# Row sums of a norm moved to token partitions by small transfers instead of transposes

## The chip, the cores and the metric

The kernel runs on one core of one Trainium2 chip. The metric is the device time of one execution in microseconds; the runs before the change have a median of 970.58 us (970.48 to 973.71, three runs).

## The reference

One encoder layer is applied to two token sequences (256 and 2048 tokens, 1024 features). Cut to what matters here:

```python
h = rms_norm(x, g_pre)
q, k, v, z_a, u_f, z_f = split(h @ w_in)                     # 512 columns each
y_a = neighbourhood_attention(q, k, v, rpb)                  # 8 heads of 64
y_f = fourier_mix(u_f, w_fourier, b_fourier)
mixed = concatenate([rms_norm(y_a, g_na) * silu(z_a), rms_norm(y_f, g_f) * silu(z_f)])
out = mixed @ w_out
return x + rms_norm(out, g_post)

def rms_norm(x, g):                                          # over the features of a token
    return x * rsqrt(mean(x * x, axis=-1) + 1e-6) * g
```

The change concerns the two norms of `y_a` and `y_f`. Each needs, for every one of the 2304 tokens, the sum of 512 squares and from it the factor 1/sqrt(sum/512 + eps).

## The kernel before, in words

The tokens are 18 tiles of 128. Both `y_a` and `y_f` are held with features on partitions and tokens along the row; the squares are added up over four blocks of 128 features into `ysq` (attention) and `sqs` (Fourier part), both 128 x 2304. So the sum over features is a sum over partitions, which TensorE makes with a matmul against ones. The factor is wanted with one token per partition (`invf`, `inva`: 128 x 18, a column for each tile), since the product with `w_out` leaves tokens on partitions and the factor is applied when PSUM is emptied (`f_evac` L1456, `evac` L1675).

The attention stage runs from about 615 to 865 us of the span. Its loop (L1577) runs over 36 groups, k = 2 to 36; the order of every engine is written out by hand, one queue per engine in the order of the code (a manual schedule for ACT, DVE, POOL, SP and PE). One turn of the loop does for group k: the scores on TensorE (L1184), biases and maxima on DVE (L1206), exponentials on ACT (L1211); and for group k-1: transposes of its softmax weights into two PSUM banks `ptb` (`transp`, L1502, which ACT empties at L1510 and DVE at L1512), then at the turn's end the product with v (`pv`, L1517, matmuls L1524). Between them stand the 12 matmuls of a half tile of the Fourier part's product with `w_out` (`f_mm` L1445, L1435), six before and six after the second transposes. At the turn's end SP's queue gets the loads for later groups: v and za of group k+1 (`prep_v`, L1138: L1152, L1154, L1159) and q of group k+3 (`prep`, L1125: L1135). Every DMA of the program is issued from SP's queue but three; eight semaphores are used in turn, so a DMA also waits until the one eight places before it has landed.

The norm's factors are made at eight places in this loop. The table `NT` (L1551) names the turn and the tiles:

```python
NT = {4: range(2, 4), 8: range(4, 8), 10: range(8, 12), 11: range(12, 16), 12: range(16, 18),
      32: range(4), 34: range(4, 8), 36: range(8, 12)}
```

At the end of turn k-1 `norm_sums` (L1479) makes the sums of up to four tiles, each with ones of 32 columns, side by side into 32 rows each of the bank `ptb[0]` (L1482), and ACT copies them to SBUF (L1484). In the middle of turn k, between the first six `w_out` matmuls and the second transposes, `norm_turn` (L1487) transposes that copy on TensorE (L1491), so that each tile's sums become a column, and `rsq_ops` (L1379) makes the factor: logarithm and exponential on ACT (L1381, L1382), and a Newton step on DVE (L1383; L1386 to L1388 a little later, by `run_later`). For k below 32 the factors are `invf`, and from 32 on `inva`.

The last stage (L1738) runs over the 18 tiles: the attention part's product with `w_out`, residual and store. In its second turn (j = 1) `a_norm` (L1495) makes the sums of the last six tiles of `inva`, one matmul pair for each tile with the squares as weights and one column of ones (L1498), which leaves tokens on partitions at once.

Of the kernel before, what the change touches and what calls it, by code (L numbers as in the profile page):

```python
# [10 lines left out]
F32 = mybir.dt.float32  # L11
# [157 lines left out]
def build(tc, A, O):  # L169
    nc = tc.nc  # L170
# [23 lines left out]
    ident = cst.tile([128, 128], F32, name="ident")  # L194
    ones = cst.tile([128, 1], F32, name="ones")
# [7 lines left out]
    invf = cst.tile([128, 18], F32, name="invf")  # L203
    inva = cst.tile([128, 18], F32, name="inva")
# [9 lines left out]
    ps = es.enter_context(tc.tile_pool(name="ps", bufs=3, space=PSUM))  # L214
# [503 lines left out]
    for c in range(3, 6):  # L718
# [7 lines left out]
        if c == 4:  # L726
# [5 lines left out]
            for k in range(KC):  # L732
                for t in range(2):
                    ts = slice(128 * t, 128 * t + 128)
# [25 lines left out]
    for b in range(16):  # L760
# [13 lines left out]
        if 2 <= b < 8:  # L774
            x, y = divmod(b, 2)
# [7 lines left out]
        p = mmt(512)[:, :TP]  # L783
# [3 lines left out]
        o = st.tile([128, 256], F32, tag="f", name="f", bufs=3)  # L787
        if kind % 2:
            i, d = p, o
        else:  # L790
            i = p.rearrange("p (b r c) -> p b r c", b=2, c=32)
# [47 lines left out]
    for i in range(16):  # L839
# [48 lines left out]
        for j in range(7):  # L888
# [29 lines left out]
            if sg == 0:  # L918
                x, y = divmod(7 * (pr - 1) + j, 14)
# [205 lines left out]
    def prep(g):  # L1125
        pr, ts = g["pr"], g["ts"]
        g["qh"] = jl.tile([128, 256], F32R, tag="qh", name="qh", bufs=4)
        g["ql"] = jl.tile([128, 256], F32R, tag="ql", name="ql", bufs=4)
        if g["R"] is None:
            q = qD[pr, :, ts].rearrange("p (b x) -> p b x", b=2)  # L1130
        else:
            sg, x = divmod(g["R"], 2)
            t0 = TP + 1024 * sg + 512 * g["hc"]
            q = qD[pr, :, t0:t0 + 512].rearrange("p (b x) -> p b x", b=2)[:, :, 128 * x:128 * x + 128]
        nc.sync.dma_start(g["ql"].bitcast(F32).rearrange("p (b x) -> p b x", b=2), q)  # L1135
# [243 lines left out]
    def rsq_ops(dst, ssum, n, scale):  # L1379
        l, y, s, t = [sm.tile([128, 8], F32, tag="d" + x, name="d" + x, bufs=1)[:, :n] for x in "lyst"]  # L1380
        nc.scalar.activation(l, ssum, AF.Ln, scale=scale, bias=epst)  # L1381
        nc.scalar.activation(y, l, AF.Exp, scale=-0.5)  # L1382
        V.tensor_scalar(s, ssum, -0.5 * scale, -0.5 * EPS, ALU.mult, ALU.add)  # L1383

        def second():
            V.tensor_tensor(out=t, in0=y, in1=y, op=ALU.mult)  # L1386
            V.tensor_tensor(out=t, in0=t, in1=s, op=ALU.mult)
            V.scalar_tensor_tensor(out=dst, in0=t, scalar=1.5, in1=y, op0=ALU.add, op1=ALU.mult)  # L1388

        later.append(second)  # L1390
# [85 lines left out]

    nsb = []

    def norm_sums(sq, ts):  # L1479
        n = 32 * len(ts)  # L1480
        for x, t in enumerate(ts):
            nc.tensor.matmul(ptb[0][32 * x:32 * x + 32, :128], ones32, sq[:, t * 128:t * 128 + 128], start=True, stop=True)  # L1482
        o = sm.tile([128, 128], F32, name="nsb", bufs=1)[:n]
        nc.scalar.copy(o, ptb[0][:n, :128])  # L1484
        nsb.append(o)

    def norm_turn(dst, ts):  # L1487
        o = nsb.pop()
        n = 32 * len(ts)
        p = ps.tile([128, 128], F32, tag="c", name="pn", bufs=1)[:, :n]  # L1490
        nc.tensor.transpose(p, o, ident[:n, :n])  # L1491
        ts = slice(ts[0], ts[-1] + 1)
        rsq_ops(dst[:, ts], p[:, ::32], ts.stop - ts.start, 1.0 / 512)

    def a_norm(ds):  # L1495
        p = ps.tile([128, 128], F32, tag="c", name="pna", bufs=1)
        for j, d in enumerate(ds):
            nc.tensor.matmul(p[:, j:j + 1], ysq[:, d["t"] * 128:d["t"] * 128 + 128], ones, start=True, stop=True)  # L1498
        n = len(ds)
        rsq_ops(inva[:, ds[0]["i"]:ds[0]["i"] + n], p[:, :n], n, 1.0 / 512)  # L1500

    def transp(g, b):  # L1502
        ch = g["ch"][b]
# [69 lines left out]
    prep_v(G[2])  # L1573
    prep(G[4])
    ones32 = sm.tile([128, 32], F32, name="ones32", bufs=1)
    nc.vector.memset(ones32, 1.0)
    for k in range(2, len(G) + 1):  # L1577
        pr, i = divmod(k, 9)
        g, f = G[k] if k < len(G) else None, G[k - 1] if k else None
        if pr < 3:  # L1580
            if i == 3:
                KK[pr + 1] = load_k(pr + 1)
                for x in range(2):
                    fetch_k(KK[pr + 1], pr + 1, x)
            if i == 7:
                load_t(pr + 1, 0)
        if 0 < pr < 4 and i == 0:
            load_t(pr, 1)
        if pr < 4 and i == 3:
            load_t(pr, 2)  # L1590
        if k == 9:
            nc.sync.dma_start(gpb, pbc(A["gpost"]))
        if k == 23:
            wp = pt.enter_context(tc.tile_pool(name="wp", bufs=1, side="right"))
            WO.extend(wp.tile([128, 4, D], F32R, name="w0%d" % x) for x in range(2))
        if 24 <= k < 32:
            y = k - 24
            nc.sync.dma_start(WO[y % 2][:, y // 2].bitcast(F32), woD[0, y % 2, y // 2])
        x = k // 2 + 1
        if g:  # L1600
            scores(g)
            if 2 < k < 34 and k % 2 == 0:
                ys_mul(ftiles[x])
                if x + 1 < 18:
                    ys_load(ftiles[x + 1])
            bias_max(g, 0, 0)
            exps(g, 0, 0)
            bias_max(g, 0, 1)
            bias_max(g, 1, 0)
        if f:  # L1610
            transp(f, 0)
        if g:
            exps(g, 0, 1)
            bias_max(g, 1, 1)
            exps(g, 1, 0)
            f_mm(k, range(6))
            soft(g, 0)
            exps(g, 1, 1)
        else:
            a_mm(atiles[0], 0, range(6))  # L1620
        if k in NT:
            norm_turn(invf if k < 32 else inva, NT[k])
        if f:
            transp(f, 1)
        if g:
            if k + 1 < len(G):
                split_q(G[k + 1])
            soft(g, 1)
            if k == 2:
                ys_mul(ftiles[x])  # L1630
                ys_load(ftiles[x + 1])
        run_later()
        for v, x0, x1 in YSQ.get(k, []):
            nc.scalar.activation(v[:, x0:x1], v[:, x0:x1], AF.Square)
            V.tensor_tensor(out=sqs[:, x0:x1], in0=sqs[:, x0:x1], in1=v[:, x0:x1], op=ALU.add)
        if g:
            f_mm(k, range(6, 12))
        else:
            a_mm(atiles[0], 0, range(6, 12))
        if pr < 3 and i == 8:  # L1640
            mask_p(pr + 1)
        if k % 2 and x < 18:
            ys_split(ftiles[x])
        if pr < 3 and i in (5, 6, 7, 8):
            split_k(KK[pr + 1], i - 5)
        if k == 34:
            ys_split(atiles[0])
        if g:
            f_evac(k)
        if f:  # L1650
            pv(f)
        if k + 1 in NT:
            norm_sums(sqs if k < 31 else ysq, NT[k + 1])
        if k == 12:
            pq_.close()
        if k + 1 < len(G):
            prep_v(G[k + 1])
        if k + 3 < len(G):
            prep(G[k + 3])
        if k == 28:  # L1660
            xk = [kp.tile([128, T], F32, tag=x, name="xk") for x in ("kh", "kl")]
        if 32 <= k < 36:
            x, d = k - 32, atiles[k - 32]
            d["xt"] = xk[x // 2][:, x % 2 * D:x % 2 * D + D]
            nc.sync.dma_start(d["xt"], A["xn"][d["t"] * 128:d["t"] * 128 + 128, :])
        if k == 32:
            ys_load(atiles[0])
        if k in (34, 35):
            ys_load(atiles[k - 33])
            of_load(atiles[k - 34])  # L1670
        if k == 36:
            ys_split(atiles[1])
# [65 lines left out]
    for j, d in enumerate(atiles):  # L1738
        if j + 3 < 18:
            ys_load(atiles[j + 3])  # L1740
        for x in range(2, 5) if j == 0 else (j + 4,):
            if x < 18:
                of_load(atiles[x])
                if x > 3:
                    xt_load(atiles[x])
        if j:
            a_mm(d, 0)
        if j == 1:
            a_norm(atiles[12:])
            run_later()  # L1750
        a_evac(d, 0)
        if j + 2 < 18:
            y_hi(atiles[j + 2])
        if j == 0:
            for n in range(2):
                nc.scalar.copy(ptb[n], gpb[:, n * 512:n * 512 + 512])
        if j == 17:
            last_tile(d, atiles[16])
            break
        if j:  # L1760
            factor(atiles[j - 1])
            for n in range(2):
                residual(atiles[j - 1], n)
        a_mm(d, 1)
        a_evac(d, 1)
        part_sum(d["sa"])
        guess(d)
        if j + 2 < 18:
            y_lo(atiles[j + 2])
# [16 lines left out]
```

## Time and profile before

| what | value |
|---|---|
| median of the runs | 970.58 us (970.48 to 973.71) |
| the profiled execution: time, span | 971.28 us, 969.5 us |
| mean granted TensorE clock | 0.998 |
| DMA | 279.37 MB in 146382 packets, 288 GB/s |
| attention stage, 615 to 869 us: PE / DVE / ACT / POOL busy | 253.0 / 163.0 / 169.5 / 169.5 of 254.0 us |
| the same stage: share of the DMA engines | 0.86 |
| transposes L1491 | 8, 270 to 273 ns each |
| sums L1482 | 56 matmuls for 28 tiles, 272 to 297 ns each |
| sums L1498 | 12 matmuls for 6 tiles |
| ACT copies L1484 | 8, 247 to 261 ns each |

A float32 matmul that isn't a transpose stands as two instructions in the trace. Durations of matmuls overlap, so the chain of work that ended last tells better than they do what an instruction adds. A row of a timeline is: start in us, length in us, engine, line, operation, tiles written and read, shapes, count, and in brackets the idle time before it with what ended it. For SP's queue (SPq) the length is the time of issuing a DMA, not that of its transfer.

### The profile page before, as it was taken

Reading aid. Unit: us, or ns where it says so; the run is one execution under the profiler, and the core shown is the slowest. Engines: PE = TensorE matmul, PEld = TensorE weight load, DVE = VectorE, ACT = ScalarE, POOL = GpSimd, SP = SyncE. Lnnn points to the kernel's source line nnn. Section 1 sums busy time; section 2 is a strip of 40 time slices with the busy share of each in tenths; the row PEclk is TensorE's granted clock in tenths of the full one; section 3 lists DMA queues with packets and bytes.
Section 4 is the critical chain, followed back from the end, with each engine's and each line's share of the span. In section 5 each row is a group of like instructions: output and inputs, shape, how many; then the busy total and the mean of one; then the engine's idle time right before and its main releaser. Section 6 shows DMA issues by size and latency. Waiting matters only on the chain.

```text
span 969.5 us, 17019 instructions
## 1 busy us (share of the span) xinstructions
PE 959.5 (99%) x5745; PEld 800.4 (83%) x5745; DVE 705.4 (73%) x1306; ACT 496.1 (51%) x1078; POOL 429.8 (44%) x400
## 2 busy tenths in 40 slices
PE   9999999999999999999999999999999999999997
PEld 7889988888888888888888879878787888878886
DVE  6758988687886777797877345776765656649997
ACT  6835676423334533233344256677666676744443
POOL 3100002464751202665655033567677686524544
PEclk9999999999999999999999999999999999999999
DMA  9898796557748997599889898689877998979993
GB/s 334 309 380 316 256 346 245 199 198 261 294 186 353 343 413 258 198 364 344 308 297 333 294 324 328 190 272 297 264 227 249 278 302 283 293 253 324 344 338 133
DMA packets 146382, 279.37 MB, mean 288 GB/s; under 512 B 13730, under 2 KB 84216, under 8 KB 142904
## 3 DMA queue, kind: packets, MB, share of 16 engines
q1 hardware_dynamic: 145864, 277.89, 81.9%
q8 instruction: 46, 0.75, 0.3%
q10 hardware_dynamic: 432, 0.39, 0.1%
q14 instruction: 40, 0.33, 0.1%
HBM read 183.85 MB, written 101.52 MB: 294 GB/s over the span
## 4 chain that ended last, share of the span: by engine, by line
PE 94%; DMA 1%; DVE 1%; SPq 1%; issue 1%; ACT 1%; POOL 1%; DVEq 0%; ACTq 0%; POOLq 0%
PE po L1435 20%; PE mm L165 18%; PE mm L164 17%; PE mm L166 17%; PE pv L1524 5%; PE ptb L1508 5%; PE s L1184 4%; PE pab L1024 2%; DMA ut<-uN 1%; PE py L164 1%; PE py L166 1%; PE py L165 1%; SPq L367 1%; DMA gpre<-gpre 0%; PE ppq L1062 0%
## 5 line engine op out<-in xcount | busy, mean ns | idle before, releaser
L164 PE MATMUL mm<-xh,wa 128*128 128x512 f32 x448 | 174.4, 389 | 0.0
L165 PE MATMUL mm<-xl,wa 128*128 128x512 f32 x448 | 174.3, 389 | 0.0
L166 PE MATMUL mm<-xh,wa 128*128 128x512 f32 x448 | 174.3, 389 | 0.0
L536 POOL TENSOR_TENSOR ws<-wr 128x512 f32<-128x512 f32 x16 | 23.5, 1468 | 228.0 <-DMA wr<-wz 224.0
L1218 POOL TENSOR_SCALAR w<-w,m 128x465 f32<-128x465 f32 (+9 forms) x136 | 85.2, 639 | 44.1 <-DVE m L1215 34.1
L164 PEld LDWEIGHTS mm<-xh,wa 128*128 128x128 f32 x448 | 84.1, 188 | 17.7
L166 PEld LDWEIGHTS mm<-xh,wa 128*128 128x128 f32 x448 | 84.1, 188 | 17.4
L165 PEld LDWEIGHTS mm<-xl,wa 128*128 128x128 f32 x448 | 84.1, 188 | 17.4
L1435 PE MATMUL po<-wo,yh 128*128 128x512 f32 x272 | 90.5, 414 | 0.0
L551 DVE TENSOR_TENSOR wa<-wr,wa 128x512 fp32r<-128x512 f32 x60 | 69.3, 1162 | 27.2 <-ACT wa L550 27.0
L1435 PE MATMUL po<-w,yh 128*128 128x512 f32 x280 | 86.7, 391 | 0.0
L1211 ACT ACTIVATE w<-w,m 128x465 f32<-128x465 f32 (+9 forms) x136 | 78.3, 579 | 15.5 <-DVE m L1206 15.5
L1206 DVE CUSTOM_DVE_ANT_1 w<-s,tb 128x465 f32<-128x465 f32 (+8 forms) x124 | 61.2, 531 | 9.7 <-PE s L1184 9.2
L165 PE MATMUL mm<-vl,xh 128*128 128x512 f32 x168 | 65.6, 390 | 0.2 <-DVE vl L482 0.2
L166 PE MATMUL mm<-vh,xl 128*128 128x512 f32 x168 | 65.4, 389 | 0.0
L164 PE MATMUL mm<-vh,xh 128*128 128x512 f32 x168 | 65.4, 389 | 0.0
L589 POOL TENSOR_TENSOR mt<-mt,rmask 128x880 f32<-128x880 f32 (+2 forms) x24 | 50.8, 2131 | 32.1 <-DVE mt L585 19.8
L877 DVE TENSOR_TENSOR f<-u,mm 128x512 f32<-128x512 f32 x64 | 43.5, 680 | 29.2 <-PE mm L166 24.3
L1435 PEld LDWEIGHTS po<-w,yh 128*128 128x128 f32 x280 | 52.3, 188 | 10.9 <-issue 0.2
L1508 PE MATMUL ptb<-ident,w 128*120 128x128 f32 (+8 forms) x422 | 58.9, 277 | 1.0 <-ACT nsb L1484 0.9
L550 ACT CAST wa<-wr 128x512 fp32r<-128x512 f32 x60 | 36.4, 617 | 44.8 <-PE mm L166 19.3
L1508 PEld LDWEIGHTS ptb<-ident,w 128*120 128x120 f32 (+8 forms) x422 | 47.2, 140 | 13.8 <-issue 8.0
(263 smaller groups left out, 2391.8 us busy)
## 6 DMA issues: line engine op xcount, KB each, us to landing
wr<-wz SPq DMA_DIRECT2D x48, 512.0 KB
vl<-sD SPq DMA_DIRECT2D x20, 512.0 KB
xm<-xm SPq DMA_DIRECT2D x9, 1024.0 KB
oD<-ofs SPq DMA_DIRECT2D x18, 512.0 KB
of<-oD SPq DMA_DIRECT2D x18, 512.0 KB
yr<-yD SPq DMA_DIRECT2D x34, 256.0 KB
zD<-f SPq DMA_DIRECT2D x16, 512.0 KB
woD<-wo SPq DMA_DIRECT2D x16, 512.0 KB
```

The source lines that it names most:

```text
L164: nc.tensor.matmul(out, lh, rh, start=first, stop=False)
L165: nc.tensor.matmul(out, lh, rl, start=False, stop=False)
L166: nc.tensor.matmul(out, ll, rh, start=False, stop=last)
L551: nc.vector.tensor_tensor(out=o[:, 1], in0=src, in1=o[:, 0].bitcast(F32), op=ALU.subtract)
L589: nc.gpsimd.tensor_tensor(out=o, in0=i, in1=rmask[:, m0:m0 + n].unsqueeze(2).to_broadcast([128, n, 80]), op=ALU.add)
L877: nc.vector.tensor_tensor(out=dst(f, b), in0=src(uu[u]), in1=src(p), op=op)
L1206: nc.vector.tensor_tensor_reduce(out=rows(g["w"][b][:, h, :n], w), in0=rows(g["s"][2 * b + h][:, :nr * sw(w)], sw(w))[:, :, :w], in1=tv, s ...
L1211: nc.scalar.activation(w, w, AF.Exp, bias=m[:, h:h + 1], scale=-1.0, accum_out=m[:, 2 + h:3 + h])
L1218: nc.gpsimd.tensor_scalar(w, w, m[:, 4 + h:5 + h], 1.0, ALU.mult, ALU.mult)
L1435: nc.tensor.matmul(p, (d["l"] if x == 2 else d["h"])[:, c], w(n, int(x == 1), c), start=j == 0, stop=j == 11)
L1508: nc.tensor.transpose(ptb[h][:nk, j * 128:j * 128 + 128], g["w"][b][:, h, c0:c0 + nk], ident)
L1524: nc.tensor.matmul(p[hs, b], g["v"][:nk, v, hs], g["pt"][b][:nk, h, j * 128:j * 128 + 128], start=j == 0, stop=j == len(ch) - 1)
```

## The change

The transposes are gone. At the end of turn k-1, behind `prep_v` and `prep`, `norm_turn` issues from SP's queue one DMA for each tile: one row of the copied sums (128 numbers in one partition) goes to a column of a new tile `ssum` (128 x 18), one number for each partition, SBUF to SBUF. In turn k, at the place of the transposes, `norm_root` makes the factor from `ssum`. The last six tiles' sums are made like the others, four in turn j = 1 and two in turn j = 2 of the last stage, each with its copy and its DMAs, and their factor in turn j = 4. There are 34 such DMAs in all. The copy's tile keeps one buffer.

```diff
-    def norm_sums(sq, ts):
+    def norm_sums(sq, ts, p=None):
+        p = ptb[0] if p is None else p
         n = 32 * len(ts)
         for x, t in enumerate(ts):
-            nc.tensor.matmul(ptb[0][32 * x:32 * x + 32, :128], ones32, sq[:, t * 128:t * 128 + 128], start=True, stop=True)
-        o = sm.tile([128, 128], F32, name="nsb", bufs=1)[:n]
-        nc.scalar.copy(o, ptb[0][:n, :128])
-        nsb.append(o)
-
-    def norm_turn(dst, ts):
-        o = nsb.pop()
-        n = 32 * len(ts)
-        p = ps.tile([128, 128], F32, tag="c", name="pn", bufs=1)[:, :n]
-        nc.tensor.transpose(p, o, ident[:n, :n])
+            nc.tensor.matmul(p[32 * x:32 * x + 32, :128], ones32, sq[:, t * 128:t * 128 + 128], start=True, stop=True)
+        o = sm.tile([128, 128], F32, tag="nsb", name="nsb", bufs=1)
+        nc.scalar.copy(o[:n], p[:n, :128])
+        nsb.append((ts, o))
+
+    def norm_turn():
+        while nsb:
+            ts, o = nsb.pop(0)
+            for x, t in enumerate(ts):
+                nc.sync.dma_start(ssum[:, t:t + 1], o[32 * x:32 * x + 1, :])
+
+    def norm_root(dst, ts):
         ts = slice(ts[0], ts[-1] + 1)
-        rsq_ops(dst[:, ts], p[:, ::32], ts.stop - ts.start, 1.0 / 512)
-
-    def a_norm(ds):
-        p = ps.tile([128, 128], F32, tag="c", name="pna", bufs=1)
-        for j, d in enumerate(ds):
-            nc.tensor.matmul(p[:, j:j + 1], ysq[:, d["t"] * 128:d["t"] * 128 + 128], ones, start=True, stop=True)
-        n = len(ds)
-        rsq_ops(inva[:, ds[0]["i"]:ds[0]["i"] + n], p[:, :n], n, 1.0 / 512)
+        rsq_ops(dst[:, ts], ssum[:, ts], ts.stop - ts.start, 1.0 / 512)
+
+    def a_norm(ts):
+        norm_sums(ysq, ts, ps.tile([128, 128], F32, tag="c", name="pna", bufs=1))
+        norm_turn()
...
+    ssum = sm.tile([128, 18], F32, name="ssum", bufs=1)
...
         if k in NT:
-            norm_turn(invf if k < 32 else inva, NT[k])
+            norm_root(invf if k < 32 else inva, NT[k])
...
         if k + 3 < len(G):
             prep(G[k + 3])
+        norm_turn()
...
-        if j == 1:
-            a_norm(atiles[12:])
+        if j in (1, 2):
+            a_norm(range(4 * j + 8, min(4 * j + 12, 18)))
+        if j == 4:
+            norm_root(inva, range(12, 18))
             run_later()
```

## The prediction

> **What bounds the kernel now.** I read the page's busy shares first, then its chain that ended last, then pieces of that chain around one use of the changed code, and last the queues of SyncE (SP) and ScalarE (ACT) at the same place.
>
> ```profile
> span 969.5 us, 17019 instructions
> PE 959.5 (99%) x5745; PEld 800.4 (83%) x5745; DVE 705.4 (73%) x1306; ACT 496.1 (51%) x1078; POOL 429.8 (44%) x400
> PE 94%; DMA 1%; DVE 1%; SPq 1%; issue 1%; ACT 1%; POOL 1%; DVEq 0%; ACTq 0%; POOLq 0%
> ```
>
> TensorE is busy in 99% of the span and holds 94% of the chain. So an instruction taken from TensorE is worth about its place in the chain, and whatever makes TensorE wait is paid in full, for it has no idle time in which to catch up. Pieces of the chain around the root at k=4, then one sums piece and one transpose of the root at k=10, then the late norm of six tiles (start us, length us, what):
>
> ```profile
> 633.02 1.39 PE po L1435 x6
> 634.42 0.20 PE pn L1491
> 634.62 1.02 PE ptb L1508 x8
> 635.64 1.40 PE po L1435 x6
> 637.04 1.68 PE pv L1524 x28
> ...
> 674.97 0.35 PE ptb L1482 x8
> ...
> 678.34 0.11 PE pn L1491
> ...
> 865.16 5.71 PE po L1435 x24
> 870.87 1.23 PE pna L1498 x12
> ```
>
> The pieces stand end to end: the transposes L1491 and the late sums L1498 really are on the path that sets the end.
>
> **What goes.** Eight transposes L1491. One of two tiles (64 rows) takes 0.20 us of the chain, one of four tiles 0.11; two roots have two tiles and six have four: 2 x 0.20 + 6 x 0.11 = 1.06 us. The twelve L1498 matmuls (1.23 us) become one sum of four tiles, 0.35 by the L1482 piece, and one of two; I take the same 0.35 for it as an upper bound, since it has half the matmuls. That saves 1.23 - 0.70 = 0.53. Together **-1.6 us**. The sums' copies to SBUF stay where they were; one ACT copy of the late norm comes twice (0.26 us each, in a stage with ACT far from full) and costs nothing as long as TensorE leads there, as it does in these pieces; if not, 0.26.
>
> **What comes.** The path of a norm was: sums on TensorE, copy by ACT, transpose on TensorE, logarithm by ACT (L1381). It becomes: sums, copy, 2 or 4 transfers from SP's queue, logarithm. In the changed kernel's instruction order the transfers stand in SP's queue behind the loads for later groups (v, za, ql) that the same iteration issues, and the logarithm stands in ACT's queue where it stood. It now waits for the landing of all of its transfers. Behind it in ACT's queue stand the exponential and the copy L1510 of transposed weights to SBUF, for which TensorE's pv waits; behind the matching VectorE instruction L1383 stands the other half of that copy, L1512. So a late landing stops ACT, DVE and, within half a microsecond, TensorE. At k=4 (ACT and DVE rows, then SP's queue at the same time, then what ended SP's and ACT's waits):
>
> ```profile
> 631.85 0.25 ACT L1484 COPY nsb<-ptb 64x128 f32<-64x128 f32 x1
> 635.28 0.24 ACT L1381 ACTIVATE dl<-pn,epst 128x2 f32<-128x2 f32 x1
> 635.66 0.57 ACT L1510 COPY pt<-ptb 120x512 f32<-120x512 f32 x1
> 635.68 0.69 DVE L1512 COPY pt<-ptb 120x512 f32<-120x512 f32 x1
> ```
>
> ```profile
> 634.50 3.92 SPq L1159 DMA_DIRECT2D za<-zD  x1
> 638.47 0.57 SPq L1135 DMA_DIRECT2D ql<-qD  x1
> 640.37 0.37 SPq L1405 DMA_DIRECT2D yr<-yD  x1
> 641.53 0.36 SPq L1408 DMA_DIRECT2D yz<-zD  x1
> ```
>
> ```profile
> SPq L1405 <- DMA tb<-tD: 1.3, 1, 1.3
> SPq L1408 <- DMA oD<-ofs: 0.7, 1, 0.7
> ```
>
> ```profile
> 645.04 0.41 ACT L1163 CAST qh<-ql 128x256 fp32r<-128x256 f32 x1 [1.48 <-DMA ql<-qD]
> ```
>
> The copy ends at 632.10 and the logarithm starts at 635.28, so the new transfers have 3.2 us of cover. But SP is still pushing out za when the logarithm is due, and ql leaves only by 639.04. The next two transfers of before had to wait for earlier ones to land, until 640.37 and 641.53; the two new ones take just these places. And ql, issued at 638.47, landed at about 645.0, where ACT was waiting for it: 6.6 us. Transfers of one queue land in the order of issue in such a row of waits, so I let the two small ones land just behind it, at 645.2. The slack of TensorE: L1512 ends at 636.37 and pv starts at 636.97 to 637.04, so 0.5 us after the semaphore. Loss at k=4: 645.2 - 635.28 - 0.5 = **9.4 us**; from below, 641.53 + 2.0 (the shortest landing that I allow, see below) gives 643.5 and 7.7 us.
>
> For the other seven roots these are SP's last instruction ahead of the new transfers and the logarithm, k=8, 10, 11, 12, 32, 34; at k=36 nothing long stands ahead, and the transfers wait for the copy itself:
>
> ```profile
> 664.28 0.43 SPq L1135 DMA_DIRECT2D ql<-qD  x1
> 678.94 0.43 SPq L1135 DMA_DIRECT2D ql<-qD  x1
> 685.50 0.43 SPq L1135 DMA_DIRECT2D ql<-qD  x1
> 690.82 0.43 SPq L1135 DMA_DIRECT2D ql<-qD  x1
> 834.72 0.43 SPq L1135 DMA_DIRECT2D ql<-qD  x1
> 845.41 0.34 SPq L1159 DMA_DIRECT2D za<-zD  x1
> ```
>
> ```profile
> 665.40 0.25 ACT L1381 ACTIVATE dl<-pn,epst 128x4 f32<-128x4 f32 x1
> 678.83 0.25 ACT L1381 ACTIVATE dl<-pn,epst 128x4 f32<-128x4 f32 x1
> 685.33 0.25 ACT L1381 ACTIVATE dl<-pn,epst 128x4 f32<-128x4 f32 x1
> 692.56 0.24 ACT L1381 ACTIVATE dl<-pn,epst 128x2 f32<-128x2 f32 x1
> 832.87 0.25 ACT L1381 ACTIVATE dl<-pn,epst 128x4 f32<-128x4 f32 x1
> 847.87 0.25 ACT L1381 ACTIVATE dl<-pn,epst 128x4 f32<-128x4 f32 x1
> 858.90 0.26 ACT L1484 COPY nsb<-ptb 128x128 f32<-128x128 f32 x1
> 861.69 0.26 ACT L1381 ACTIVATE dl<-pn,epst 128x4 f32<-128x4 f32 x1 [1.29 <-PE pn L1491]
> ```
>
> At three of them (k=10, 11, 32) ql is issued after the logarithm had already run. An issue takes 0.43 us, so the last of four leaves 1.29 us behind the first. The landing of a 512-byte row spread to 128 partitions is not in the trace. From below: the kernel's last store, and the span's end behind it,
>
> ```profile
> 966.51 0.33 SPq L1713 DMA_DIRECT2D yo<-xt  x1
> ```
>
> leave at most 969.5 - 966.5 = 3.0 us for a landing in an empty queue together with the closing of the program; I take two thirds of it, 2.0, as the lower end. From above the 6.6 us of ql in a full queue. SP was not held up for microseconds at these places as it was at k=4, so I take 3.0, near the row of the empty queue. Loss = end of the row ahead + 1.29 (or 0.43) + 3.0 - logarithm - 0.5:
> k=8: 664.71 + 4.29 - 665.90 = 3.1. k=10: 679.37 + 4.29 - 679.33 = 4.3. k=11: 685.93 + 4.29 - 685.83 = 4.4. k=12: 691.25 + 3.43 - 693.06 = 1.6. k=32: 835.15 + 4.29 - 833.37 = 6.1. k=34: 845.75 + 4.29 - 848.37 = 1.7. k=36: 859.16 + 4.29 - 862.19 = 1.3.
> With k=4 that is **+31.9 us**. With 2.0 instead of 3.0 at seven roots, and 7.7 at k=4, it is 23.2; with 4.5 at seven it is 42.4, and 6.6 everywhere 57. The last norm (tiles 12 to 17) is read two tiles after the second of its sums; a tile's 24 matmuls take 5.7 us in the pieces above, so it has some 11 us and waits for nothing: 0. If that cover were gone, it would cost what the root at k=36 does, 1.3.
>
> The Trainium skill's page "DMA: Bandwidth & Descriptors" (Anatomy of one DMA) gives a small transfer some 2.0 us of fixed cost, most of it the receipt of the write. By that figure the sum would be at its lower end, 7 us less at the seven roots, as an estimate; no run shown here has the transfer alone.
>
> **Two corrections.** A long wait of TensorE lowers its clock. The two windows after its last matmul (PEclk is the third number from the end):
>
> ```profile
> 962.80:965.90 3.10, 0.00 (x0) 0.00 (x0) 2.80 (x11) 1.02 (x6) 1.48 (x2) 1.00 0.45 169
> 966.10:969.40 3.30, 0.00 (x0) 0.00 (x0) 0.38 (x1) 0.00 (x0) 0.00 (x0) 0.50 0.43 159
> ```
>
> After some 3.3 us of idle the granted clock was 0.50. The losses at k=4 and k=32 are clearly longer; if the clock takes as long to come back, 3.3 us of work at half speed lose about 2 us each: +4 (0 to +10, the upper end if k=10 and k=11 also fall into it). The page "TensorE: Matmul & The Clock Gate" (Part 1) of the Trainium skill states a free-running window of 3.4 us for both directions, with which the trace's 3.3 agrees. The other way: while TensorE stands still, queued transfers land, so the root after a loss finds an emptier queue; k=10, 11 and 12 come close together. I take -3 (-6 to 0).
>
> **Sum.** -1.6 + 31.9 + 4.0 - 3.0 = +31.3 us. The profiled execution took 971.28 us with a span of 969.5; its sum is 1002.6. The median of the runs shown is 970.58, 0.7 lower: **1002 us**.
>
> **Rivals.**
> (A) The wait is hidden and only the saving is left: 970.6 - 1.6 = 969.0 us, the other side. The mechanism is that each row is in flight while ACT still has softmax work ahead of the logarithm. It decides for this when the last transfer lands within 3.2 + 0.5 us of the copy. For it speaks that cover; against it that at k=10, 11, 32 and 4 SP has not even issued the load ahead of the transfers when the logarithm is due. The Trainium skill states on its page "DMA: Bandwidth & Descriptors" (Rules for kernel authors) that a transfer issued early and waited for late overlaps its fixed cost; by that rule alone this case would come out.
> (B) Only the plain latency is paid: SP's lag at k=4 and k=32 dissolves (its backlog shifts with the other losses), so that k=4 loses what k=12 does, 1.6, and k=32 what k=8 does, 3.1; the sum falls by 10.8 to 21.1, no wait is long enough for the clock, and 970.6 + 21.1 - 1.6 - 1.0 (of the emptier queue) = 989 us. For it: five of the eight places show no long SP row. Against it: k=4 comes before any other loss, so nothing can dissolve its lag.
> (C) The 34 new transfers themselves lengthen the queue (they hold places that later loads wait for, as the two SP waits above show), and landings are 4.5 us rather than 3.0: 42.4 + 8 of clock - 3 - 1.6 = +45.8, 1016 us.
> That the change doesn't do what it says I exclude: in the changed kernel's order of instructions the transposes are gone, and the logarithm waits for transfers.
>
> **How the numbers follow.** Forecast 0.56, B 0.25, C 0.12, A 0.04, and 0.03 for a loss and a gain that cancel within 0.5% (4.9 us, about what a measurement of this kernel can tell from no change). So faster 0.04, same 0.03, slower 0.93. The range has to reach B's and C's times: 984 to 1018 us, from the lower end of the landings without a clock loss (23.2 - 1.6 - 6 = +15.6, 986) to a little above C.
>
> **What would show it.** Right: L1381 shows idle time in front of it ended by a DMA of ssum at all eight roots, longest at k=4 and next at k=32; pv L1524 waits for the copy of pt behind it; TensorE's busy share falls to about 96%; a granted clock of 0.5 shows in the windows after k=4. SP's first ssum issue stands right behind ql. Wrong: no DMA in front of L1381 (A), equal waits of 2 to 3 us (B), or loads of v and kl that TensorE itself waits for (C). The forecast fails most easily in the landing time, which no row shows, and in k=4, a third of the sum.

## The result, and the profile after

The changed kernel takes **1004.86 us** (median of 6 runs, 1002.04 to 1006.05). The kernel before took 970.64 beside it (median of 6, 970.21 to 973.71). The ratio is 1.0345, with a 95% interval of 1.0329 to 1.0361: it became slower by 34 us. The profiled execution took 1004.12 us with a span of 1002.3, which is 32.8 us more than the span of before.

These are the changed kernel's span, the busy time of its engines, the granted clock in 40 slices, the DMA packets, and the shares of the chain that ended last:

```profile
span 1002.3 us, 17074 instructions
PE 967.0 (96%) x5737; PEld 804.2 (80%) x5737; DVE 703.3 (70%) x1306; ACT 497.7 (50%) x1080; POOL 428.1 (43%) x400
PEclk9999999999999999999999999798999999899999
DMA packets 151278, 279.39 MB, mean 279 GB/s; under 512 B 18626, under 2 KB 89112, under 8 KB 147800
PE 87%; DMA 6%; ACT 2%; DVE 2%; SPq 1%; issue 1%; POOL 0%; DVEq 0%; ACTq 0%; POOLq 0%
```

TensorE no longer fills the span: 96% where it had 99%. DMA is now 6% of the chain and ACT 2%; both had 1%. The clock has dents in three slices, and roots of the norms stand in each of them. The waits sit on one line of each engine. First what ended ACT's idle time ahead of the logarithm L1381 (us, times), then the group of TensorE's pv matmuls, whose last two numbers are the idle time ahead of it and what ended it:

```profile
  DMA ssum<-nsb: 35.9, 8
```

```profile
L1524 PE MATMUL pv<-pt,v 120*64 120x128 f32 (+9 forms) x880 | 59.8, 284 | 24.3 <-ACT pt L1510 24.3
```

All eight roots in the loop wait for their transfers, 35.9 us on ACT, and 24.3 us of it reach TensorE, which waits for the copy L1510 that stands behind the logarithm. The eight logarithms in order (k=4, 8, 10, 11, 12, 32, 34, 36) and the late one, which waits for nothing:

```profile
643.48 0.30 ACT L1381 ACTIVATE dl<-ssum,epst 128x2 f32<-128x2 f32 x1 [8.90 <-DMA ssum<-nsb]
678.15 0.30 ACT L1381 ACTIVATE dl<-ssum,epst 128x4 f32<-128x4 f32 x1 [3.19 <-DMA ssum<-nsb]
696.89 0.30 ACT L1381 ACTIVATE dl<-ssum,epst 128x4 f32<-128x4 f32 x1 [4.76 <-DMA ssum<-nsb]
707.32 0.30 ACT L1381 ACTIVATE dl<-ssum,epst 128x4 f32<-128x4 f32 x1 [3.89 <-DMA ssum<-nsb]
716.20 0.29 ACT L1381 ACTIVATE dl<-ssum,epst 128x2 f32<-128x2 f32 x1 [0.94 <-DMA ssum<-nsb]
863.91 0.30 ACT L1381 ACTIVATE dl<-ssum,epst 128x4 f32<-128x4 f32 x1 [8.38 <-DMA ssum<-nsb]
881.03 0.30 ACT L1381 ACTIVATE dl<-ssum,epst 128x4 f32<-128x4 f32 x1 [1.61 <-DMA ssum<-nsb]
896.55 0.30 ACT L1381 ACTIVATE dl<-ssum,epst 128x4 f32<-128x4 f32 x1 [4.22 <-DMA ssum<-nsb]
921.01 0.28 ACT L1381 ACTIVATE dl<-ssum,epst 128x6 f32<-128x6 f32 x1
```

The same waits as TensorE has them, at the pv matmuls of k=4, 8, 10, 11, 32 and 36 (k=12 and 34 have none):

```profile
644.54 1.98 PE L1524 MATMUL pv<-pt,v 120*64 120x128 f32 x16 [7.86 <-ACT pt L1510]
679.11 0.88 PE L1524 MATMUL pv<-pt,v 128*64 128x128 f32 x12 [2.04 <-ACT pt L1510]
697.73 0.69 PE L1524 MATMUL pv<-pt,v 80*64 80x128 f32 x8 [3.79 <-ACT pt L1510]
708.28 1.40 PE L1524 MATMUL pv<-pt,v 120*64 120x128 f32 x12 [2.41 <-ACT pt L1510]
864.87 1.55 PE L1524 MATMUL pv<-pt,v 120*64 120x128 f32 x12 [7.02 <-ACT pt L1510]
897.50 0.88 PE L1524 MATMUL pv<-pt,v 96*64 96x128 f32 x12 [1.17 <-ACT pt L1510]
```

And the stretches after the waits in which the granted clock was 0.50 (length, TensorE's busy time; the clock is the third number from the end):

```profile
644.50:650.40 5.90, 5.86 (x36) 4.87 (x37) 3.70 (x11) 2.40 (x6) 2.38 (x3) 0.50 0.41 95
681.20:684.60 3.40, 3.40 (x12) 2.68 (x11) 1.70 (x10) 1.56 (x7) 2.81 (x2) 0.50 0.91 335
698.20:701.60 3.40, 3.40 (x29) 2.63 (x25) 2.12 (x8) 1.31 (x5) 2.35 (x4) 0.50 0.38 117
708.50:711.90 3.40, 3.40 (x26) 2.61 (x24) 1.56 (x3) 1.66 (x5) 3.27 (x5) 0.50 0.44 149
862.10:868.90 6.80, 4.04 (x25) 3.11 (x26) 3.16 (x11) 1.83 (x6) 2.75 (x4) 0.50 0.17 48
```

TensorE worked 5.86 + 3 x 3.40 + 4.04 = 20.1 us at half clock; by arithmetic that work would have taken 10 us less at full clock. So the account of this one execution is 24.3 of waits + 10 of half clock - 1.6 saved (the prediction's figure) = 32.7, where the spans differ by 32.8. The profile's own sums say much the same: TensorE's idle time rose by 25.3 us (from 969.5 - 959.5 to 1002.3 - 967.0) and its busy time by 7.5. That the account agrees to a tenth is chance: its 1.6 was not measured, and the first root of all, ahead of everything that the change touches, already starts 0.8 us earlier in the changed kernel (611.9) than in the one before (612.7).

### The profile page after: what moved, and what is told of

It reads as the page before. It is cut to its first block, busy times and chain, and to the rows that moved or that the text cites. A ratio compares the mean times of both kernels' runs of the same rounds, so it can differ in the third digit from the quotient of the medians.

```text
span 1002.3 us, 17074 instructions
## 1 busy us (share of the span) xinstructions
PE 967.0 (96%) x5737; PEld 804.2 (80%) x5737; DVE 703.3 (70%) x1306; ACT 497.7 (50%) x1080; POOL 428.1 (43%) x400
## 2 busy tenths in 40 slices
DMA packets 151278, 279.39 MB, mean 279 GB/s; under 512 B 18626, under 2 KB 89112, under 8 KB 147800
## 4 chain that ended last, share of the span: by engine, by line
PE 87%; DMA 6%; ACT 2%; DVE 2%; SPq 1%; issue 1%; POOL 0%; DVEq 0%; ACTq 0%; POOLq 0%
PE po L1435 17%; PE mm L165 17%; PE mm L166 17%; PE mm L164 17%; PE pv L1524 5%; PE ptb L1508 4%; PE s L1184 4%; DMA wr<-wo 2%; DMA ssum<-nsb 2%; PE pab L1024 2%; DMA oD<-ofs 1%; PE py L164 1%; SPq L1492 1%; PE py L166 1%; PE py L165 1%
## 5 line engine op out<-in xcount | busy, mean ns | idle before, releaser
L1211 ACT ACTIVATE w<-w,m 128x465 f32<-128x465 f32 (+9 forms) x136 | 78.3, 579 | 19.5 <-DVE m L1206 19.4
L1524 PE MATMUL pv<-pt,v 120*64 120x128 f32 (+9 forms) x880 | 59.8, 284 | 24.3 <-ACT pt L1510 24.3
L1524 PEld LDWEIGHTS pv<-pt,v 120*64 120x64 f32 (+9 forms) x880 | 48.9, 140 | 38.9 <-ACT pt L1510 26.0
L589 POOL TENSOR_TENSOR mt<-mt,rmask 128x880 f32<-128x880 f32 (+2 forms) x24 | 50.3, 2109 | 32.7 <-DVE mt L585 20.4
```

The costliest lines, as they stand in the source:

```text
L589: nc.gpsimd.tensor_tensor(out=o, in0=i, in1=rmask[:, m0:m0 + n].unsqueeze(2).to_broadcast([128, n, 80]), op=ALU.add)
L1211: nc.scalar.activation(w, w, AF.Exp, bias=m[:, h:h + 1], scale=-1.0, accum_out=m[:, 2 + h:3 + h])
L1524: nc.tensor.matmul(p[hs, b], g["v"][:nk, v, hs], g["pt"][b][:nk, h, j * 128:j * 128 + 128], start=j == 0, stop=j == len(ch) - 1)
```

## Experiments

The theory: what costs is the path of a root, the transfer's place in SP's queue plus its landing, since the logarithm is due before it. The rivals: the 34 transfers themselves load the queue (C of the prediction), or the half clock behind the waits carries much of the loss. In the expectations, T is the theory. A ratio stands with its 95% interval, against the kernel before.

**Transfers that nobody reads.** The kernel before, all its transposes kept, and the 28 transfers of the loop issued where the changed kernel has them:

```diff
+    def norm_out():
+        while out:
+            ts, o = out.pop(0)
+            for x, t in enumerate(ts):
+                nc.sync.dma_start(ssum[:, t:t + 1], o[32 * x:32 * x + 1, :])
...
         if k + 3 < len(G):
             prep(G[k + 3])
+        norm_out()
```

> The kernel before with its transposes, and the in-loop transfers (28 of the 34) issued as in the changed kernel, but read by nobody. Theory T (the loss is ACT's wait for late landings, passed on to TensorE): nobody waits, so 971 us, within 1.5 of before. Rival R (the transfers themselves load the queue and delay the loads behind them): most of the loss stays, 985 us or more.

Measured 977.54 us, ratio 1.0055 (1.0038 to 1.0072). The theory missed, by 5 us. What ACT's copy to nsb waited for in this kernel:

```profile
687.25 0.27 ACT L1484 COPY nsb<-ptb 128x128 f32<-128x128 f32 x1 [4.20 <-DMA ssum<-nsb]
```

A transfer holds its source too. There is one buffer nsb, and the next sums' copy had to wait 4.20 us until the transfers of the last had read it; TensorE stood 3.99 us behind it. (In the changed kernel that copy waited once as well, 3.8 us.) So a second kernel puts the first five roots' sums into slices of another tile that nothing overwrites in time, and is otherwise the same:

```diff
-        o = sm.tile([128, 128], F32, name="nsb", bufs=1)[:n]
+        if sq is sqs:
+            o = y0[:n, 0, len(used) % 4]
+            used.append(o)
+        else:
+            o = sm.tile([128, 128], F32, name="nsb", bufs=1)[:n]
...
```

> Transposes kept and 28 transfers read by nobody, as in the run before it of this kind, but the first five roots' sums are copied to memory of their own (a tile that is free by then), so that no copy has to wait for transfers out of the same buffer. That wait (4.2 us at one copy, and 3.4 us at half clock behind it) is theory T's account of the 5.4 us that the earlier run lost: 971 to 973 us. Rival R (28 more transfers in the queue cost by themselves): 976 us or more again.

Measured 974.49 us, ratio 1.0030 (1.0014 to 1.0046). The time lies between the two: 2.9 us remain that the transfers cost though nobody reads them. Where they go is not shown. In its profile one wait of TensorE stands out, 1.0 us for a load of v at 707.7, but the profiled execution, at 971.99 us, was one of the quickest of this kernel. The rival has a true part of some 3 us (1.4 to 4.5) out of 34; the rest comes from waiting for the result.

**Ahead in SP's queue.** The changed kernel with its transfers issued ahead of the loads for later groups:

```diff
         if k + 1 in NT:
             norm_sums(sqs if k < 31 else ysq, NT[k + 1])
+            norm_turn()
...
             prep(G[k + 3])
-        norm_turn()
```

> The changed kernel with the transfers issued ahead of the loads of v, za and q instead of behind them. Theory T: the loss per root falls by the time SP spends on those loads. Where SP has no backlog a root of four tiles still lands about 1.9 + 2.05 us after the copy against a cover of 3.7, so about 0.5 is left, and at k=4 and k=32, where earlier large transfers are still in flight, some 6.5 and 3.5 us are left: with the clock about 985 us (978 to 990). Rival L (plain latency of a transfer is the cost, the place in the queue is not): little gain, 998 us or more.

Measured 991.46 us, ratio 1.0197 (1.0174 to 1.0221): just above the range of 978 to 990 us. 43% of the loss goes, by the ratios (0.0148 of 0.0345). ACT's waits, and the first transfers at k=4 in SP's queue with the logarithm behind them:

```profile
  DMA ssum<-nsb: 22.5, 6
```

```profile
631.19 1.19 SPq L1492 DMA_DIRECT2D ssum<-nsb  x2
```

The waits fall from 35.9 to 22.5 us, so the place in the queue counted for 13 of them. Why the rest is 6 us more than expected shows in part at k=4: the pair leaves at 631.19, and the first logarithm that reads ssum starts only at 640.4 (its line's first start). Being first at SP didn't make it land early, for loads that SP had issued before were still on their way.

**From ACT's queue.** The transfers of the loop issued by ACT right behind its copy, so that nothing of SP's stands ahead:

```diff
-    def norm_turn():
+    def norm_turn(q=nc.sync):
...
-                nc.sync.dma_start(ssum[:, t:t + 1], o[32 * x:32 * x + 1, :])
+                q.dma_start(ssum[:, t:t + 1], o[32 * x:32 * x + 1, :])
...
+            norm_turn(nc.scalar)
...
-        norm_turn()
```

> The changed kernel with the transfers of the roots in the loop issued from ACT's own queue, right behind its copy. They pass SP's backlog, but ACT issues for 0.5 to 0.6 us each, 2.3 us for a root of four tiles, ahead of the exponentials. Theory T: k=4 and k=32 lose most of their 8 and 7 us; the last transfer lands about 2.3 + 2.1 us after the copy, so 1 to 2 us are left at each root of four: 978 us (974 to 985). If the data movers serve all queues in the order of issue, the backlog stays ahead of them, and k=4 and k=32 wait as long as with SP's queue ahead of the loads: 988 us or more.

Measured 997.58 us, ratio 1.0272 (1.0243 to 1.0301); the alternative came true. ACT's queue in this kernel, at k=4 and at k=32:

```profile
631.06 1.31 ACTq L1492 DMA_DIRECT2D ssum<-nsb  x2
...
640.19 0.30 ACT L1381 ACTIVATE dl<-ssum,epst 128x2 f32<-128x2 f32 x1 [4.80 <-DMA ssum<-nsb]
```

```profile
844.96 4.80 ACTq L1492 DMA_DIRECT2D ssum<-nsb  x4
849.81 0.58 ACT L1211 ACTIVATE w<-w,m 128x345 f32<-128x345 f32 x1 [8.31 <-DMA ssum<-nsb]
```

The pair at k=4 left 7.3 us earlier than in the changed kernel, and its logarithm started 3.3 us earlier, at 640.19, the same time as in the kernel that issues them ahead in SP's queue (640.4). So it is the transfers under way, not SP's order, that set this landing. At k=32 the four issues took ACT 4.80 us, because they too had to wait for places (the trace has the last one leave at 849.28, when a transfer oD<-ofs had landed at 849.26), and ACT's softmax exponentials L1211 stood behind them. The Trainium skill says on its page "DMA: Bandwidth & Descriptors" (Issuing engines are not separate DMA queues) that transfers run on the same 16 engines whichever engine issues them, and that a second issuer saves only issuing time; these two rows agree with it.

**Half a turn earlier.** Sums and transfers moved to the middle of the turn, with a PSUM buffer of their own; the root at k=4 keeps its transpose:

```diff
...
+        if k > 3 and k + 1 in NT:
+            norm_sums(sqs if k < 31 else ysq, NT[k + 1], ps.tile([128, 128], F32, tag="c", name="pns", bufs=1))
+            norm_turn()
...
```

> The changed kernel with the sums and transfers half a turn earlier for all roots in the loop but k=4, which keeps its transpose; each transfer then has about a full turn (7 us) to land. Theory T: no wait is left and only the saving of TensorE remains: 969.2 us (968.5 to 970.5). Rival R (the transfers load the queue): above 972 us.

Measured 976.78 us, ratio 1.0045 (1.0027 to 1.0063), 7.6 us above the expected 969.2. ACT still waits at three roots, and at k=32 TensorE does too; the four issues there, with SP's row ahead, and TensorE's wait:

```profile
829.91 0.33 SPq L1607 DMA_DIRECT2D w<-woD  x1
831.09 2.45 SPq L1492 DMA_DIRECT2D ssum<-nsb  x4
```

```profile
837.33 1.32 PE L1532 MATMUL pv<-pt,v 120*64 120x128 f32 x12 [1.97 <-ACT pt L1518]
```

SP's lag at k=32 is longer than the lead gained. The next kernel keeps the transposes at k=4 and k=32 and moves only the other six (its edit against the kernel just above):

```diff
-            if k == 4:
-                turned(invf, NT[k])
+            if k in (4, 32):
+                turned(invf if k < 32 else inva, NT[k])
...
-        if k > 3 and k + 1 in NT:
+        if k not in (3, 31) and k + 1 in NT:
```

> Transposes at k=4 and at k=32, where SP's queue is behind; sums and transfers half a turn earlier at k=8, 10, 11, 12, 34 and 36; the last six tiles as in the changed kernel. Theory T: the one wait that was left with k=32 in the earlier group (3.3 us of ACT, 2.0 of TensorE) goes, and 1.1 us of TensorE's work is saved: 0.5 to 1.5 us below the kernel before. Rival R: 3 us or more above it.

Measured 971.57 us, ratio 0.9998 (0.9986 to 1.0010). With this lead the loss is gone, within 1 us. But the gain of 0.5 to 1.5 us that was expected is not there either, though six transposes and the late sums are saved. What ended ACT's waits at the roots in this kernel:

```profile
  DMA ssum<-nsb: 4.8, 2
```

So half a turn was not enough everywhere: at k=11 and k=36 ACT still waited, 1.73 and 3.04 us, and TensorE's pv stood 0.68 and 0.28 us behind it. Against the 1.1 us of TensorE's work that was saved this counts. The load of the transfers, seen above, can take part too; neither was measured by itself here.

**The late norm alone.** The kernel before, with the last six tiles' sums made four side by side and brought over by transfers, as in the change:

```diff
...
-        if j == 1:
-            a_norm(atiles[12:])
+        if j in (1, 2):
+            a_norm(range(4 * j + 8, min(4 * j + 12, 18)))
+        if j == 4:
+            rsq_ops(inva[:, 12:], ssum[:, 12:], 6, 1.0 / 512)
```

> The kernel before with only the last six tiles changed: sums of four and of two tiles side by side, copies, transfers, root at j=4. Theory T: 0.5 us faster (0.2 to 0.8), hidden otherwise: 0.9995 of before. If the stage has a wait for them: slower by 1 us or more.

Measured 970.52 us, ratio 0.9989 (0.9980 to 0.9999): about 1 us faster, just outside no change. Its pieces of the chain at the two sums:

```profile
873.69 0.36 PE pna L1498 x8
...
879.72 0.34 PE pna L1498 x4
```

0.36 + 0.34 = 0.70 us of sums, where the one piece of before has 1.23. It is the only version here with an interval below that of the kernel before.

**Filling TensorE's waits.** The changed kernel with matmuls that nobody reads ahead of pv, so that the clock stays up (about as many as fit into each wait):

```diff
+    FILL = {4: 60, 8: 12, 10: 28, 11: 16, 32: 56, 36: 6}
...
+        for x in range(FILL.get(G.index(g) + 1, 0)):
+            nc.tensor.matmul(p, wo1[0][0][:, 0, :128], wo1[0][0][:, 0, :256], start=True, stop=True)
```

> The changed kernel with idle matmuls on TensorE ahead of the products with v at k=4, 8, 10, 11, 32 and 36, a little shorter than TensorE's waits there, so that the waits stay and the idle time goes; their results are overwritten. If the half clock after the waits costs what its 20 us of busy time at 0.5 suggest, about 996 us (994 to 999). If TensorE's waits alone make the loss: 1005 us, no change.

Measured 1003.3 us, ratio 1.0321 (1.0296 to 1.0345): nearer to "nothing". Core and clock, first of the changed kernel, then of this one, and what ended ACT's waits in this one:

```profile
core 0: 1002.3 us, clock 0.985
```

```profile
core 0: 1000.8 us, clock 0.997
```

```profile
  DMA ssum<-nsb: 39.7, 8
```

The half clock is gone, and the span fell by 1.5 us, not by 9. ACT's waits grew from 35.9 to 39.7. That fits an account that is argued here and not shown: with TensorE faster between the roots, each next root comes due earlier, while the landings follow SP and the transfers. How much of the missing gain is that, and how much is filling that ran past a landing, isn't told apart. The waits that were left ahead of pv here:

```profile
L1527 PE MATMUL pv<-pt,v 120*64 120x128 f32 (+9 forms) x880 | 57.9, 277 | 7.1 <-ACT pt L1510 7.1
```

With the filling, 178 matmuls that take 0.12 us each in their rows of the trace, that is 21.4 + 7.1 = 28.5 us in place of 24.3. It accounts for 4.2 of the 8.5 us between the arithmetic's 10 and the 1.5 that came back; the rest stays open.

**One root at a time.** To have the price of one wait without its neighbours, only the root at k=4 goes by transfers; the other seven keep their transposes, and the late norm is as changed:

```diff
+            if k == 4:
                 norm_root(invf if k < 32 else inva, NT[k])
+            else:
+                turned(invf if k < 32 else inva, NT[k])
...
+        if k == 3:
             norm_turn()
```

> Theory: each wait costs its own idle time of TensorE plus the work done at half clock behind it, and nothing later gives it back. Here only the root at k=4 goes by transfers (its sums and transfers where the changed kernel has them); the other seven in the loop keep their transposes; the six late tiles are done as in the changed kernel, 1 us less. From the changed kernel's trace: 7.9 us idle before the second half of pv, then some 5.9 us of work at half clock, 2.9 us. 970.6 - 1 + 7.9 + 2.9 = 980.4, range 978 to 983. The prediction on record priced this root at 9.4, that is 979. Rival: the seven other roots take part of it, because the lag in SP's queue is theirs together: then the wait at k=4 alone is shorter and the time is under 977.

Measured 979.83 us, ratio 1.0083 (1.0058 to 1.0107). The same with k == 32 and k == 31 in the two lines:

> Only the root at k=32 goes by transfers, at the changed kernel's place; the others keep their transposes. Theory of additive waits: 7.0 us idle and 4.0 us of work at half clock, 2.0 us, as in the changed kernel: 970.6 - 1 + 7.0 + 2.0 = 978.6, range 976 to 981; the prediction on record had 6.1 for it, 976. Rival: the wait at k=32 in the changed kernel was long because the transfers stand behind lagging loads that belong to the transposes removed before: then it is under 4 us here and the time under 975.

Measured 978.85 us, ratio 1.0070 (1.0046 to 1.0093). TensorE's longest wait in the one and in the other (us, times, longest):

```profile
PE pv L1532 <- ACT pt L1518: 7.6, 1, 7.6
```

```profile
PE pv L1532 <- ACT pt L1518: 7.3, 1, 7.3
```

Alone, the two waits are as long as in the changed kernel (7.9 and 7.0). So neither is a shared lag: each belongs to its own place in SP's queue, and the waits add up. At k=32 the last piece ahead of the logarithm is a landing of 2.05 us:

```profile
839.26 0.47 SPq L1492
...
839.78 2.05 DMA ssum<-nsb
```

The queue was not empty then: seven transfers issued before it were still under way and landed one after another, from 839.97 to 841.48 by the semaphores of the trace. In the changed kernel the last transfer of a root took 2.03 to 2.05 us from issue to landing at k=8, 10, 32 and 34, and the shortest of any trace here is 1.9. The Trainium skill's page "DMA: Bandwidth & Descriptors" (Anatomy of one DMA) has some 2.0 us of fixed cost. It gives them for transfers that GpSimd issues, which the prediction left out; these transfers, issued by SP and ACT, come near them.

Last, the kernel with only k=4 by transfers, with 52 filling matmuls ahead of its pv:

```diff
+        for x in range(52 if g is G[3] else 0):
+            nc.tensor.matmul(p, wo1[0][0][:, 0, :128], wo1[0][0][:, 0, :256], start=True, stop=True)
```

> As the kernel with the root at k=4 alone by transfers, and 52 matmuls that nobody reads before this turn's pv, 6.2 us at the 0.12 us that each took in the kernel that filled all waits. They keep TensorE busy while it would wait. Theory: there is no later wait here that could grow, so the half clock's 2.9 us come back: 977.5, range 976 to 979.5, with the granted clock at 0.99 or more behind k=4. Rival: the half clock is hidden by other work in this stretch, and the time is that of the kernel without the filling, within 1 us.

Measured 980.00 us, ratio 1.0088 (1.0065 to 1.0110): the time of the kernel without the filling. But the trace shows a gain that then goes. The kept logarithms that read a transpose (k=8 to k=36) and the first root of all, without and with the filling (the times are the first and last start):

```profile
L1381 ACT ACTIVATE dl<-pn,epst x7: 243/246/263, 674.8 to 871.0; 128x4 f32<-128x4 f32 x6, 128x2 f32<-128x2 f32 x1
...
L1381 ACT ACTIVATE dl<-pfn,epst x1: 262/262/262, 613.2 to 613.2; 128x2 f32<-128x2 f32 x1
```

```profile
L1381 ACT ACTIVATE dl<-pn,epst x7: 243/246/263, 672.8 to 871.8; 128x4 f32<-128x4 f32 x6, 128x2 f32<-128x2 f32 x1
...
L1381 ACT ACTIVATE dl<-pfn,epst x1: 262/262/262, 612.8 to 612.8; 128x2 f32<-128x2 f32 x1
```

From the first root to k=8 it is 674.8 - 613.2 = 61.6 us without and 672.8 - 612.8 = 60.0 with the filling, 1.6 us less. The kernel without it worked for 3.40 us at half clock behind this wait, and not for the 5.9 that the expectation took from the changed kernel:

```profile
645.60:649.00 3.40, 3.40 (x26) 3.00 (x28) 2.25 (x6) 1.26 (x3) 2.38 (x3) 0.50 0.64 166
```

By arithmetic that is 1.7 us, so in these two profiles the half clock cost what it should at this place. From the first root to k=36 it is 257.8 and 259.0: the gain is gone, behind three short waits near k=30 to 33 that only the filled kernel's profile has (0.6, 0.4 and 0.2 us for other operands, 1.2 of the 2.8 that were lost there). Whether the faster part brought these about, or they are the scatter of one execution, one profile of each doesn't tell, and the intervals don't resolve 1.6 us.

## Why the prediction was right, and where it was not

The forecast of 1002 us was 3 us low, and its mechanism holds: the logarithm came to wait for its transfers at all eight roots, longest at k=4, next at k=32, and TensorE stood behind ACT's copy for pv. Busy share 96%, as said. Step by step:

- **What goes, -1.6.** Right where it can be seen: the late sums take 0.70, and that alone moved the time by about 1 us. The transposes' 1.06 was never seen as a gain; the load of the transfers (2.9 us when nobody reads them) is larger.
- **The waits.** The prediction's loss plus its 0.5 of slack is a forecast of ACT's wait. Its eight values are 9.9, 3.6, 4.8, 4.9, 2.1, 6.6, 2.2 and 1.8, in sum 35.9; measured were 8.90, 3.19, 4.76, 3.89, 0.94, 8.38, 1.61 and 4.22, in sum 35.9 too. Of the 4.22 at k=36 ACT had waited 1.29 in the kernel before as well (for the transposes), so 34.6 were added. Root by root the forecast was 1.8 too low at k=32, 1.1 too low at k=36, and too high by 0.4 to 1.2 at five of the others.
  At k=4 the mechanism is as forecast: by the semaphores of the trace the pair landed just behind ql (642.98, then 643.19 and 643.40). At the other seven roots the sum came out well partly by luck, since its two terms were off in opposite directions. The landing of 3.0 us was too long: the last transfer took 2.0 to 2.2 us at k=8, 10, 12, 32 and 34, 3.1 at k=11 and 3.5 at k=36, 2.4 in the mean. The issues were taken too short: one takes 0.59 us and not 0.43, so the last of four left 1.8 to 2.3 us behind the first, not 1.29. The pieces of the chain at k=32 and k=36:

```profile
861.76 2.05 DMA ssum<-nsb
...
892.97 3.47 DMA ssum<-nsb
```

  At k=32 three of the four transfers had to wait for a place, the third until a load of v landed at 861.16, which the prediction had seen at k=4 alone; and SP's row ahead of them stood 3.1 us behind the time at which the logarithm was due, where it was 1.9 in the kernel before.
- **The slack of TensorE, 0.5.** This step was wrong. From ACT's waits to TensorE's it is 8.90 - 7.86 = 1.04 at k=4, 1.15 at k=8, 0.97 at k=10, 1.48 at k=11, 1.36 at k=32 and, without the 1.29 that it had before, 1.76 at k=36. The prediction measured from the last copy to the start of pv, but pv begins with the half whose copy is already there, and waits in its middle:

```profile
635.80 0.88 PE L1524 MATMUL pv<-pt,v 120*64 120x128 f32 x12
```

  These twelve matmuls ran ahead of the wait at k=4. So 24.3 us of the 35.9 reached TensorE, not 31.9.
- **An emptier queue, -3.** k=10, 11 and 12 were forecast to profit. Their ACT waits are 9.6 in sum, where 11.8 was priced without it: -2.2, within its range. That an emptier queue brought this isn't shown, for at k=11 and k=12 the overlong landing would do the same. The wait at k=32, as long alone as with the other roots, shows that a far one doesn't profit.
- **The clock, +4.** The size was wrong: 10 us by arithmetic from the windows of the profile. The prediction let only k=4 and k=32 fall to half clock, because it took 3.3 us of idle for it; its range reached to 10 for the case that k=10 and k=11 fall too, as they did. The waits of 2.04 at k=8 and 2.41 at k=11 were enough, each with its window of half clock of 3.4 us. But taking it away gave back 1.5 us, so its price as a change that one can make is far below its 10.
- The slack and the queue made the forecast of the waits 28.9 where 24.3 came, and the clock 4 where 10 came. The two misses nearly cancel, and the total owes part of its closeness to that luck.
- **The rivals.** (A), the waits hidden, came in no kernel but the one with half a turn of lead at six roots, and there not at all of them. (B), the lag at k=4 and k=32 dissolving, fell: these two are 15 of the 24 us. (C) is true in kind, but its 2.9 us are a small part and the landings did not become 4.5 us long for it.

## What to carry to other kernels

A transfer in place of a short instruction of the busiest engine removes a tenth or two of a microsecond and adds an issue, a place in a queue and a landing of 2 us at best, 4 to 9 behind large loads in these traces; before it is made, measure how long the result can wait, from the producer's end to the consumer's start, at each place where it is used. If that lead is shorter than the queue's lag, move the producer, not the queue: half a turn of lead at six of the eight roots left no loss that could be measured here, though two of the six still waited; at all eight, another issuer or a better place in the queue repaid a fifth to two fifths. And when a wait is priced, follow it to the engine that sets the end: what that engine can still do ahead of its own wait is the slack.

## What had not been expected of the hardware

- The granted clock falls after waits of only 2 us, some 3 to 4 us after the wait began. The rows around k=8 in the changed kernel:

```profile
677.10:679.10 2.00, 0.00 (x0) 0.00 (x0) 0.90 (x5) 0.92 (x4) 0.00 (x0) 1.00 0.53 140
679.10:681.20 2.10, 2.10 (x27) 1.83 (x28) 1.31 (x4) 1.21 (x3) 1.76 (x4) 0.99 0.94 274
```

  TensorE is idle at full clock, works 2.1 us at full clock, and only then has 3.4 us at half, at work all the time. All falls lie on one grid: the stretches begin at 640.2, 681.2, 698.2, 708.5 and 862.1, and the last four are 12, 17, 20 and 65 times 3.413 us behind the first. So it depends on where a wait meets the grid: the last 3.41 us before the fall at 681.2 hold only 1.4 us of the wait at k=8. The wait of 1.17 us at k=36 brought no fall. The Trainium skill's window on the page "TensorE: Matmul & The Clock Gate" (Part 1) is 3.4 us and free-running: the length of the half-clock stretches and the grid agree, but its wording of one idle window ahead of the throttle doesn't fit a wait of 2.0 us.
- One row of 512 bytes spread over 128 partitions is 144 packets: the packets under 512 bytes rose from 13730 to 18626, by 4896, for 34 transfers. The row of before:

```profile
DMA packets 146382, 279.37 MB, mean 288 GB/s; under 512 B 13730, under 2 KB 84216, under 8 KB 142904
```

- Such a transfer keeps SP for longer than the 0.43 us of a load (shortest, median and longest in ns, first and last start):

```profile
L1492 SPq DMA_DIRECT2D ssum<-nsb x34: 469/588/631, 638.4 to 914.1; - x34
```
